# Squares summed on VectorE at the end of layer 0, their statistics between two projections, three banks for the values, other load and block orders

## The chip, the cores and the metric

One core of one Trainium2 chip. The metric is the device time of one launch in microseconds, as the median of several runs.

## What is computed

A transformer of two layers on 512 image tokens and 256 context tokens of 1024 features, all in float32. Each layer normalises, projects to queries, keys, values and a Fourier input, runs three mixers (global attention, a Fourier mix, attention in a window), projects back, and then runs a gated FFN of width 2816. The context is carried along in layer 0 only; in layer 1 it serves keys and values.

```python
def swiglu(h, w_gate, w_up, w_down):
    return (jax.nn.silu(h @ w_gate) * (h @ w_up)) @ w_down

def reference(x, c, ctx, c_ctx, w_ada, ..., g_final):
    rope = axial_rope_tables(x.shape[1])
    for l in range(DEPTH):                                  # DEPTH = 2
        update_ctx = l < DEPTH - 1
        sh1, sc1, gt1, sh2, sc2, gt2 = ...adaln(c, w_ada[l], b_ada[l])
        h = rms_norm(x, g_mix[l]) * (1 + sc1) + sh1
        hc = rms_norm(ctx, g_mix[l]) * (1 + csc1) + csh1
        qa, ka, va, fb, qc, kc, vc = mixer_inputs(h, w_in[l], q_norm[l], k_norm[l], rope)
        qac, kac, vac, fbc, qcc, kcc, vcc = mixer_inputs(hc, w_in[l], q_norm[l], k_norm[l], None)
        o = concatenate([global_attention(qa, ka, va, kac, vac), fourier_mix(fb),
                         window_attention(qc, kc, vc, kcc, vcc, sink[l])])
        x = x + gt1 * (o @ w_out[l])
        x = x + gt2 * swiglu(rms_norm(x, g_ffn[l]) * (1 + sc2) + sh2, w_gate[l], w_up[l], w_down[l])
        if update_ctx:
            ...                                             # the same for ctx
    return rms_norm(x, g_final)
```

## The kernel before

**Arithmetic.** Every float32 product is three passes of a reduced format: each operand is split into a high part and a remainder, and high times high, high times low and low times high are summed in PSUM. `split` (L95) makes the high part with a cast on ScalarE and the low part with a subtraction on VectorE; `mm3` (L89) issues the three matmuls for each pair of operands. Because both are helpers, most rows of the profile carry L89 or L95, and the names of the tiles tell the steps apart: `w` split weights, `raw` weights as loaded, `u` the product of gate and up (and other temporary tiles), `ahi`/`alo` the normalised activations, `th`/`tl` sums of them.

**Large products by seven.** The output projection and the FFN multiply 2 by 2 blocks with seven products in place of eight. The operands' sums are made on GpSimd and VectorE (`seven`, L1269 to L1313). In layer 0 the FFN keeps `u`: parts of it are written to DRAM as `uh` and `uf` and read back, and the seven products with `w_down` come at the end in the order 1, 6, 2, 7, 5, 4, 3, each over eleven panels `k` (`product`, L1453; matmuls L1462). Product 1 needs the blocks of `w_down` in `a11`; `a21` and `a22` are loaded meanwhile, and `sums_of` turns the three into the operands of later products on VectorE.

**PSUM.** There are eight banks in three pools: `lg` two tiles of two banks, `mm` three banks, `fl` one bank. A matmul that starts a new tile waits until the last reader of the tile before in that bank is done.

**The end of layer 0.** `add` (L1471) puts a finished output block into the residual `xt`, and `stat_add` squares it on ScalarE into one of two buffers `sq` and adds the square to `acc`. `stat` (L399, L400) then sums over the features with one-column matmuls, `bc` takes the reciprocal root (GpSimd, L314) and spreads it by a matmul with the identity (L413); `norm_h` makes the normalised `u` on VectorE (L430), `ahi` on ScalarE (L433) and `alo` on VectorE (L434). The tokens come in two halves of 384: the half with block 3 and the context's blocks 4 and 5 (a block is 128 tokens) is finished and normalised during product 3, the half with blocks 0 to 2 after it. The next layer's first projection of block 3 (`qkv_first`, L487 to L489) is computed in between, and the context's blocks 4 and 5 (`qkv_ctx`) after the statistics.

**Layer 1's start.** `qkv_rest` computes `va` (the values of the global attention) in three products, each in a bank handed over as an argument, then the other columns, of which `kc` also uses `fl`. Keys are rotated (L667 to L669), transposed (L589) and cast to `K1a`; queries are transposed (L750); L792 and L800 are the logits.

**Layer 1's FFN.** Eleven panels of 256 columns. Each panel runs `seven` for the gate and for up, multiplies (L1623) and splits the result `u`, in two halves `j`, and one panel later `down` multiplies it by `w_down` into `mm`, eight output blocks of six matmuls (two `j` by three).

**What sets the order.** A scheduler orders the instructions of each engine ahead of time from the order of the code and modelled times; each engine then works through its list strictly in order. `issue_after` pins what is written under it behind a named instruction. SyncE's queue issues nearly all the loads.

Of the kernel before, what the change touches and what calls it, by code (L numbers as in the profile page):

```python
# [17 lines left out]
P = 128  # L18
D = 1024
KB = D // P  # L20
# [26 lines left out]
class Builder:  # L47
# [30 lines left out]
    def mm(self):  # L78
        return self.mmp.tile([P, 512], F32, name=self.nm("mm"), tag="mm")
# [5 lines left out]
    def mm3(self, out, pairs, more=False):  # L85

        n = len(pairs)
        for i, (lh, ll, rh, rl) in enumerate(pairs):
            mm = lambda a, b, **k: self.nc.tensor.matmul(out, a, b, skip_group_check=more, **k)  # L89
            mm(lh, rh, start=(i == 0 and not more), stop=False)  # L90
            mm(lh, rl, start=False, stop=False)
            mm(ll, rh, start=False, stop=(i == n - 1))

    def split(self, hi, lo, src):
        return self.nc.scalar.copy(hi, src).ins, self.nc.vector.tensor_sub(lo, src, hi).ins  # L95
# [295 lines left out]
    def stat(self, acc, rng, ps=None):  # L391

        nc = self.nc
        r0, r1 = rng
        n = (r1 - r0) // P
        ps = self.mm() if ps is None else ps
        for t in range(n):
            o = ps[:, t : t + 1]
            nc.tensor.matmul(o, acc[:, r0 + t * P : r0 + (t + 1) * P], self.ones, start=True, stop=False)  # L399
            nc.tensor.matmul(o, self.lastsq[:, t * P : (t + 1) * P], self.ones, start=False, stop=True)  # L400
        return ps[:, 0:n]

    def stat_bc(self, acc, rng, bank=None, ps=None):
# [108 lines left out]
    def qkv_ctx(self, hi, lo, ws, h0):  # L512

        cs = slice(h0 * HD, 512)
        outs = []
        for tb in range(TBX, TB):
            ts = slice(tb * P, (tb + 1) * P)
            ps = self.mm()
            self.mm3(
                ps[:, cs], [(hi[k][:, ts], lo[k][:, ts], ws[k][0][:, cs], ws[k][1][:, cs]) for k in range(KB)]  # L520
            )
            outs.append(ps)
        return outs

    def qkv_a(self, l, hi, lo, ws, outs):

# [488 lines left out]
    def mix(self, l, hi, lo, ws, outs):  # L1015
        nc = self.nc
        full = l < DEPTH - 1
        self.qkv_tiles(full)
        krs, rms, turn = self.qkv_a(l, hi, lo, ws, outs)
        va = self.qkv_rest(l, hi, lo, "va", self.fl, self.mm, self.fl)  # L1020
        va.pop(0)()

        if full:
# [352 lines left out]
    def ffn_full(self, l, xt, hs):  # L1376
        nc = self.nc
        wg, wu = (self.a[k][l] for k in ("w_gate", "w_up"))
        wd = self.a["w_down"][l].rearrange("(p i q) c -> q p i c", i=2, q=P)
        npc = FB // 2  # L1380
# [37 lines left out]
        half = (slice(0, 512), slice(512, 1024))  # L1418
        a11 = [r[k // 4][:, k % 4] for k in range(8)] + t2[0:3]
        a22 = t2[3 : 3 + npc]  # L1420
        a21 = [act(i) for i in range(npc)]
        for k in range(0, 8, 2):
            nc.sync.dma_start(r[k // 4][:, k % 4 : k % 4 + 2], wd[:, k : k + 2, 0, half[0]])
        turn = [0]
# [46 lines left out]
        def add(v, d, r0, last=False):  # L1471

            for x0, x1, s in ((r0, min(SX, r0 + n), 0), (max(SX, r0), r0 + n, 1)):
                if x0 < x1:
                    nc.vector.scalar_tensor_tensor(
                        xt[d][:, x0:x1], v[:, x0 - r0 : x1 - r0], self.gt(l, 1, d, s), xt[d][:, x0:x1], op0=ALU.mult, op1=ALU.add
                    )
            if last:
                h = r0 // n
                self.stat_add(acc, xt[d], (r0, r0 + n), seen[h], nc.gpsimd)  # L1480
                seen[h] += 1

        def sums_of(k):

            nc.sync.dma_start(a21[k], wd[:, k, 0, half[1]])
            nc.sync.dma_start(a22[k], wd[:, k, 1, half[1]])
            nc.vector.tensor_sub(a11[k], a11[k], a21[k])
            nc.vector.tensor_add(a21[k], a21[k], a22[k])
            nc.vector.tensor_sub(a22[k], a22[k], a11[k])
# [4 lines left out]
        def behind(k):  # L1494

            if k + 4 in range(8, npc):
                nc.sync.dma_start(a11[k + 4], wd[:, k + 4, 0, half[0]])
            if k >= 4:
                sums_of(k - 4)

        half4 = range(4)
        A = [(self.mm() if i else self.fl())[:, 0:n] for i in half4]
        product(1, A, then=behind)
        for k in range(npc - 4, npc):
            sums_of(k)
        s1 = [t[:, i * n : (i + 1) * n] for t in [self.utile(F32) for _ in range(2)] for i in range(2)]
        for i in half4:
            nc.scalar.copy(s1[i], A[i])
# [45 lines left out]
        self.qkv_first(hi, lo, ws, outs, (3,))  # L1554
        for i in half4:
            add(A[i], i, n2, True)
        bc = self.stat_bc(acc, (0, n), self.fl(), self.mm())
        outs += self.qkv_ctx(hi, lo, ws, KB - 2)
        for d in (4, 5, 6, 7, 0, 1, 2, 3):
            nc.sync.dma_start(self.xsc[:, d, 0:SX], xt[d][:, 0:SX])  # L1560
        self.norm_h(hi, lo, xt, bc, (0, n), l + 1, 0, 0, room)
# [3 lines left out]
    def ffn(self, l, xt, hs):  # L1565
# [12 lines left out]
        def down(p, us, rng, s, wd2, ds=range(KB)):  # L1578
            r0, r1 = rng
            last = p == npc - 1  # L1580
            for d in ds:
                ps = self.mm()[:, 0 : r1 - r0]
                c = slice(d * P, (d + 1) * P)
                self.mm3(
                    ps,
                    [
                        (wd2[j][0][:, c], wd2[j][1][:, c], us[j][0][:, r0:r1], us[j][1][:, r0:r1])
                        for j in (1, 0)
                    ],
                )  # L1590
# [15 lines left out]
        for p in range(1, npc):  # L1606
            g = [self.utile(F32) for _ in range(2)]
            self.seven(wg[:, cols(p)], toks, n, *g, lambda o, ps: nc.scalar.activation(o, ps, AF.Silu))
            for t in (g[0][:, n : 2 * n], both(g[1])):
                nc.scalar.activation(t, t, AF.Silu)  # L1610
            wd2 = load_down(p - 1)
            down(p - 1, us, XR, 0, wd2)
            if full:
                down(p - 1, us, CR, 1, wd2)
            m = [self.utile(F32) for _ in range(2)]
            self.seven(
                wu[:, cols(p)], toks, n, *m, lambda o, ps: nc.vector.tensor_tensor(o, ps, g[0][:, 0:n], op=ALU.mult)
            )
            us = utiles()
            if p < npc - 1:  # L1620
                for j in (1, 0):
                    e = slice(0 if j else n, 2 * n)
                    nc.vector.tensor_tensor(m[j][:, e], m[j][:, e], g[j][:, e], op=ALU.mult)  # L1623
                    v = (lambda t: both(t).rearrange("p (i n) -> p i n", i=2)) if j else both
                    self.split(v(us[j][0]), v(us[j][1]), swap(m[j]) if j else both(m[j]))
                continue
            for h in range(2):
                for j in range(2):
                    a = slice((h ^ j) * n, ((h ^ j) + 1) * n)
                    o = slice(h * n, (h + 1) * n)  # L1630
                    if h or j:
                        nc.vector.tensor_tensor(m[j][:, a], m[j][:, a], g[j][:, a], op=ALU.mult)
                    self.tail = self.split(us[j][0][:, o], us[j][1][:, o], m[j][:, a])
# [179 lines left out]
```

## Time and profile before

| | |
|---|---|
| runs | 1590.9, 1590.29, 1589.07 us; median 1590.29 |
| the profiled execution | 1590.55 us, span 1588.8 us |
| mean granted TensorE clock | 0.976 |
| busy: TensorE, VectorE, ScalarE, GpSimd | 95%, 71%, 48%, 37% |
| context blocks, statistics and block 3 at layer 0's end | about 904 to 935 us |
| start of layer 1 up to its first logits | about 935 to 978 us |
| layer 1's FFN | about 1190 to 1566 us |
| product 1 of layer 0's `w_down` | about 735 to 755 us |

PE is TensorE, PEld its weight loads, DVE VectorE, ACT ScalarE, POOL GpSimd, SP SyncE. A timeline row has start, duration (of the whole row, where several instructions are gathered, "x6"), engine, line, operation, output and inputs, and in brackets the idle time before it and what ended it. A row of a group has its total and the mean of one in ns. The clock column is the share of the full TensorE clock that was granted.

### The profile page before, as it was taken

The page shows a single profiled execution, that of the slowest core. Times are in us where ns is not written, and L with a number is a line of the kernel's source. Part 1 is how long each engine was busy: PE and PEld are TensorE (multiplying, and loading weights), DVE is VectorE, ACT ScalarE, POOL GpSimd, SP SyncE. Part 2 cuts the span into 40 slices and gives each one's busy share as a digit, 9 for nine tenths or more (in the row PEclk, how much of TensorE's full clock was granted, in tenths as well). Part 3 has the DMA queues.
Part 4 walks back from the last instruction along what each step waited for, and adds up shares of the span by engine and source line. Part 5 has one row for each costly group of instructions (what it writes and reads, how often), then busy time and mean ns, then how long its engine had stood idle before and what let it go on. Part 6 is the DMA issues. An engine that isn't in the chain of part 4 may idle for free. (4 is left out here: it accounts for less than half of the span.)

```text
span 1588.8 us, 25749 instructions
## 1 busy us (share of the span) xinstructions
PE 1513.1 (95%) x9817; PEld 1383.3 (87%) x9817; DVE 1133.9 (71%) x1891; ACT 765.6 (48%) x1540; POOL 583.5 (37%) x475
## 2 busy tenths in 40 slices
PE   6989999999999999998999898999899999999997
PEld 3689977688999999998999888987799898988987
DVE  4566577753987788887587645667749777787775
ACT  4356566641744344442355424666627343443434
POOL 2163355410265655551021205453401443344432
PEclk9999999999999999999999979999999999999998
DMA  9420075851044345449973610055441423223221
GB/s 339 151 80 28 1 241 174 290 178 54 27 144 163 127 144 179 138 139 393 310 252 105 186 53 27 28 165 200 150 133 54 133 80 106 81 84 129 80 80 53
DMA packets 124842, 217.75 MB, mean 137 GB/s; under 512 B 6616, under 2 KB 83440, under 8 KB 119600
## 3 DMA queue, kind: packets, MB, share of 16 engines
q1 hardware_dynamic: 116864, 210.08, 38.5%
q0 software_dynamic: 7856, 6.04, 1.9%
q8 instruction: 77, 1.26, 0.3%
q14 instruction: 45, 0.37, 0.1%
HBM read 184.96 MB, written 31.13 MB: 136 GB/s over the span
## 5 line engine op out<-in xcount | busy, mean ns | idle before, releaser
L95 DVE TENSOR_TENSOR w<-raw,w 128x512 fp32r<-128x512 f32 (+1 forms) x334 | 316.5, 960 | 111.8 <-ACT w L95 107.1
L95 ACT CAST w<-raw 128x512 fp32r<-128x512 f32 (+1 forms) x334 | 226.5, 699 | 326.3 <-POOL raw L1277 94.4
L89 PE MATMUL mm<-u,w 128*128 128x512 f32 (+1 forms) x576 | 141.6, 387 | 15.2 <-ACT u L95 11.9
L89 PE MATMUL fl<-ahi,w 128*128 128x384 f32 (+1 forms) x640 | 154.4, 309 | 1.0 <-ACT acc L1338 0.9
L811 POOL TENSOR_TENSOR p<-p,rc 128x768 f32<-128x768 f32 (+2 forms) x84 | 112.2, 1354 | 117.0 <-DVE rc L809 108.4
L89 PE MATMUL lg<-ahi,w 128*128 128x384 f32 (+1 forms) x640 | 151.3, 312 | 1.0 <-DVE u L1300 0.9
L89 PE MATMUL lg<-th,w 128*128 128x384 f32 (+1 forms) x640 | 149.9, 309 | 1.1 <-DVE u L1401 0.7
L89 PE MATMUL fl<-w,ahi 128*128 128x256 f32 (+1 forms) x640 | 125.7, 292 | 5.9 <-DVE t L669 3.1
L89 PEld LDWEIGHTS mm<-u,w 128*128 128x128 f32 x576 | 100.3, 196 | 33.4 <-ACT u L95 13.1
L89 PEld LDWEIGHTS lg<-ahi,w 128*128 128x128 f32 x640 | 112.6, 193 | 5.0 <-ACT w L95 1.7
L89 PEld LDWEIGHTS fl<-ahi,w 128*128 128x128 f32 x640 | 112.1, 189 | 2.8 <-ACT acc L1338 1.1
L89 PEld LDWEIGHTS lg<-th,w 128*128 128x128 f32 x640 | 110.9, 189 | 2.8 <-DVE u L1401 1.1
L89 PEld LDWEIGHTS fl<-w,ahi 128*128 128x128 f32 x640 | 103.8, 197 | 7.7 <-issue 2.7
L89 PE MATMUL mm<-ahi,w 128*128 128x256 f32 (+1 forms) x448 | 107.1, 330 | 0.0
L1277 POOL TENSOR_TENSOR raw<-raw 128x512 f32<-128x512 f32 x40 | 62.2, 1556 | 103.5 <-DVE w L95 103.5
L89 PE MATMUL lg<-alo,w 128*128 128x384 f32 (+1 forms) x320 | 99.2, 311 | 0.0
L89 PE MATMUL fl<-alo,w 128*128 128x384 f32 (+1 forms) x320 | 98.7, 308 | 0.0
L89 PE MATMUL lg<-tl,w 128*128 128x384 f32 (+1 forms) x320 | 98.7, 308 | 0.0
L95 DVE TENSOR_TENSOR t<-mm,t 128x512 fp32r<-128x512 f32 x108 | 74.0, 687 | 33.1 <-ACT t L95 32.2
L1269 POOL TENSOR_TENSOR s<-raw 128x512 f32<-128x512 f32 x40 | 53.0, 1326 | 114.8 <-DMA raw<-in_w_up_dram 71.0
L89 PE MATMUL fl<-w,alo 128*128 128x256 f32 (+1 forms) x320 | 92.8, 290 | 0.0
L803 DVE TENSOR_REDUCE neg<-lg 128x1 f32<-128x768 f32 (+2 forms) x96 | 81.0, 852 | 14.6 <-PE lg L800 13.4
(352 smaller groups left out, 3957.8 us busy)
## 6 DMA issues: line engine op xcount, KB each, us to landing
raw<-in_w_ada_dram SPq DMA_DIRECT2D x40, 1024.0 KB, 4.9
raw<-in_w_gate_dram SPq DMA_DIRECT2D x22, 1024.0 KB, 5.2
raw<-in_w_up_dram SPq DMA_DIRECT2D x22, 1024.0 KB, 5.2
uh<-uh SPq DMA_DIRECT2D x44, 384.0 KB, 5.3
w<-uh SPq DMA_DIRECT2D x44, 384.0 KB, 4.6
wd<-in_w_down_dram SPq DMA_DIRECT2D x58, 256.0 KB, 5.4
raw<-in_w_down_dram SPq DMA_DIRECT2D x11, 1024.0 KB, 4.8
raw<-in_w_in_dram SPq DMA_DIRECT2D x10, 1024.0 KB, 6.2
```

The lines of the kernel that those rows point to most:

```text
L89: mm = lambda a, b, **k: self.nc.tensor.matmul(out, a, b, skip_group_check=more, **k)
L95: return self.nc.scalar.copy(hi, src).ins, self.nc.vector.tensor_sub(lo, src, hi).ins
L803: nc.vector.tensor_reduce(ng, lv, axis=AX.X, op=ALU.max, negate=True)
L811: nc.gpsimd.tensor_tensor(pt, pt, rc[:, i : i + 1].to_broadcast(list(pt.shape)), op=ALU.mult)
L1269: nc.gpsimd.tensor_add(s1, a21, a22)
L1277: nc.gpsimd.tensor_sub(a12, a12, a11)
```

## The change

1. **Adds of squares.** At the end of layer 0 the twelve adds of squares into `acc` (three after each of products 2, 5, 4 and 3) run on VectorE, not on GpSimd.
2. **Statistics between the context's blocks.** `qkv_ctx` hands over one block at a time. Block 4 comes first, then `stat`, pinned behind its last matmul, then block 5, pinned behind `stat`, then `bc`.
3. **Banks for the values in layer 1.** The three products of `va` go to `mm`, `lg` and `fl` instead of `fl`, `mm` and `fl`.
4. **Loads of w_down in layer 0.** `a21` is loaded four panels behind product 1 as before, but `a22` and the sums come six behind; and the tiles behind `a21` are taken in another order.
5. **Order of the halves.** In layer 1's FFN half `j` = 0 comes before half 1, both in the multiply and split of `u` and in the six matmuls of each `down` block.

```diff
-            mm(ll, rh, start=False, stop=(i == n - 1))
+            self.last = mm(ll, rh, start=False, stop=(i == n - 1)).ins
...
     def qkv_ctx(self, hi, lo, ws, h0):
...
-            outs.append(ps)
-        return outs
+            yield ps
...
-        va = self.qkv_rest(l, hi, lo, "va", self.fl, self.mm, self.fl)
+        va = self.qkv_rest(l, hi, lo, "va", *((self.fl, self.mm, self.fl) if full else (self.mm, self.lg1, self.fl)))
...
-        a21 = [act(i) for i in range(npc)]
+        a21 = [act(i) for i in (0, 1, 2, 3, 8, 9, 10, 4, 5, 6, 7)]
...
-                self.stat_add(acc, xt[d], (r0, r0 + n), seen[h], nc.gpsimd)
+                self.stat_add(acc, xt[d], (r0, r0 + n), seen[h])
...
         def sums_of(k):
 
-            nc.sync.dma_start(a21[k], wd[:, k, 0, half[1]])
             nc.sync.dma_start(a22[k], wd[:, k, 1, half[1]])
...
-            if k >= 4:
-                sums_of(k - 4)
+            if 4 <= k < npc + 4:
+                nc.sync.dma_start(a21[k - 4], wd[:, k - 4, 0, half[1]])
+            if k >= 6:
+                sums_of(k - 6)
...
-        for k in range(npc - 4, npc):
-            sums_of(k)
+        for k in range(npc, npc + 6):
+            behind(k)
...
-        bc = self.stat_bc(acc, (0, n), self.fl(), self.mm())
-        outs += self.qkv_ctx(hi, lo, ws, KB - 2)
+        ctx = self.qkv_ctx(hi, lo, ws, KB - 2)
+        outs.append(next(ctx))
+        with self.tc.issue_after(self.last):
+            ss = self.stat(acc, (0, n), self.mm())
+        with self.tc.issue_after(self.last):
+            outs.append(next(ctx))
+        bc = self.bc(ss, n // P, self.fl())
...
-                        for j in (1, 0)
+                        for j in range(2)
...
-                for j in (1, 0):
+                for j in range(2):
                     e = slice(0 if j else n, 2 * n)
                     nc.vector.tensor_tensor(m[j][:, e], m[j][:, e], g[j][:, e], op=ALU.mult)
```

How the instructions move. TensorE's list has the same number of matmuls in both kernels. At the end of layer 0 (`lg_9330` is the projection of block 3, of which only the last panel and a half is left; `mm_9371` before and `mm_9395` after hold the statistics; `mm_9370` is context block 4 after, `mm_9385` before) it reads before:

```order
L489 MATMUL lg_9330<-w_9323,alo_9034 128x512 [waits DVE_49]
L487 MATMUL lg_9330<-w_9323,ahi_9027 128x512 [waits Activation_49]
L488 MATMUL lg_9330<-w_9324,ahi_9027 128x512
L489 MATMUL lg_9330<-w_9323,alo_9035 128x512 [waits DVE_49]
L399 MATMUL mm_9371<-ones,acc_7581 128x1 [waits Pool_49]
L400 MATMUL mm_9371<-ones,sq_9368 128x1 [waits Activation_49]
```

And after, where nineteen more rows of `mm_9370` stand ahead of the first row shown:

```order
L89 MATMUL mm_9370<-w_9324,ahi_9026 128x128
L491 MATMUL lg_9330<-w_9323,alo_9034 128x512 [waits DVE_49]
L489 MATMUL lg_9330<-w_9323,ahi_9027 128x512 [waits Activation_49]
L490 MATMUL lg_9330<-w_9324,ahi_9027 128x512
L89 MATMUL mm_9370<-w_9323,alo_9034 128x128 [waits DVE_49]
L89 MATMUL mm_9370<-w_9323,ahi_9027 128x128 [waits Activation_49]
L89 MATMUL mm_9370<-w_9324,ahi_9027 128x128
L491 MATMUL lg_9330<-w_9323,alo_9035 128x512 [waits DVE_49]
L89 MATMUL mm_9370<-w_9323,alo_9035 128x128 [waits DVE_49]
L399 MATMUL mm_9395<-ones,acc_7581 128x1 [waits DVE_49]
L400 MATMUL mm_9395<-ones,sq_9368 128x1 [waits Activation_49]
```

All of block 4 now stands between the projection of block 3 and the statistics, which wait for VectorE in place of GpSimd. (Lines after are two higher here: L489 to L491 for L487 to L489.)

At layer 1's start on TensorE before (`fl_9757` is the third product of `va`, `fl_10072` the first of `kc`, both in the one `fl` bank):

```order
L89 MATMUL fl_9757<-w_9576,ahi_9027 128x256
L89 MATMUL fl_9757<-w_9577,ahi_9027 128x256
L89 MATMUL fl_9757<-w_9576,alo_9035 128x256
L89 MATMUL fl_10072<-w_10001,ahi_9020 128x256 [waits DVE_49,PE_49,Activation_49]
L89 MATMUL fl_10072<-w_10002,ahi_9020 128x256
```

And after, where `lg_9814` is a product of `va`:

```order
L89 MATMUL fl_10072<-w_10005,ahi_9027 128x256
L89 MATMUL fl_10072<-w_10006,ahi_9027 128x256
L89 MATMUL fl_10072<-w_10005,alo_9035 128x256
L89 MATMUL lg_9814<-w_9572,ahi_9020 128x256 [waits DVE_49,Activation_49]
L89 MATMUL lg_9814<-w_9573,ahi_9020 128x256
```

The products of `kc` have moved ahead of two of `va`, which now start in another bank.

In layer 1's FFN, at the first `down` block after a panel's product 4 of the gate, on TensorE (`u_13218` and `u_13219` are the high and low part of half 0, `u_13220` and `u_13221` of half 1; `mm_13365` and `mm_13373` the first two output blocks; `lg_13440` the next panel's first product, `w_13434` its weights) before:

```order
L89 MATMUL mm_13365<-u_13220,w_13361 128x512 [waits Activation_49]
L89 MATMUL mm_13373<-u_13220,w_13361 128x512 [waits DVE_49]
L89 MATMUL lg_13440<-ahi_9020,w_13434 128x256 [waits Activation_49]
L89 MATMUL lg_13440<-alo_9028,w_13434 128x256
L89 MATMUL mm_13365<-u_13221,w_13361 128x512 [waits DVE_49]
L89 MATMUL mm_13365<-u_13220,w_13362 128x512
```

And after:

```order
L89 MATMUL mm_13365<-u_13218,w_13357 128x512 [waits Activation_49]
L89 MATMUL mm_13365<-u_13219,w_13357 128x512 [waits DVE_49]
L89 MATMUL mm_13365<-u_13218,w_13358 128x512 [waits DVE_49]
L89 MATMUL mm_13373<-u_13218,w_13357 128x512 [waits DVE_49]
L89 MATMUL mm_13373<-u_13219,w_13357 128x512
L89 MATMUL mm_13373<-u_13218,w_13358 128x512
L89 MATMUL lg_13440<-ahi_9020,w_13434 128x256 [waits Activation_49]
L89 MATMUL lg_13440<-alo_9028,w_13434 128x256
L89 MATMUL mm_13365<-u_13220,w_13361 128x512 [waits Activation_49]
```

Six matmuls of half 0 stand ahead of the next panel's first product where two of half 1 stood. On ScalarE the cast of half 0 now comes before the two casts of `w_down`, and that of half 1 behind the cast of the next panel's weights `w_13434`, which waits for their load. Before, that cast stood behind half 1's:

```order
L95 CAST w_13337<-raw_13230 128x512 [waits DVE_49,PE_49]
L95 CAST w_13357<-raw_13355 128x1024 [waits DMAHW5_49,PE_49]
L95 CAST w_13361<-raw_13355 128x1024 [waits DVE_49,PE_49]
L95 CAST u_13220<-u_13094 128x512 [waits DVE_49,Pool_49]
L95 CAST w_13434<-raw_13431 128x512 [waits DMAHW6_49,PE_49,Activation_49]
L95 CAST u_13218<-u_13093 128x512
```

And after:

```order
L95 CAST w_13337<-raw_13230 128x512 [waits DVE_49,PE_49]
L95 CAST u_13218<-u_13093 128x512 [waits DVE_49]
L95 CAST w_13357<-raw_13355 128x1024 [waits DMAHW5_49,PE_49]
L95 CAST w_13361<-raw_13355 128x1024 [waits PE_49,Activation_49]
L95 CAST w_13434<-raw_13431 128x512 [waits DMAHW6_49,PE_49,Activation_49]
L95 CAST u_13220<-u_13094 128x512 [waits DVE_49,Pool_49]
```

Half 0's cast moves from last to second.

More of the change, by code (lines that the diff above doesn't have):

```diff
@@ L399, in stat @@
             nc.tensor.matmul(o, acc[:, r0 + t * P : r0 + (t + 1) * P], self.ones, start=True, stop=False)
-            nc.tensor.matmul(o, self.lastsq[:, t * P : (t + 1) * P], self.ones, start=False, stop=True)
+            self.last = nc.tensor.matmul(
+                o, self.lastsq[:, t * P : (t + 1) * P], self.ones, start=False, stop=True
+            ).ins
         return ps[:, 0:n]
@@ L514, in qkv_ctx @@
         cs = slice(h0 * HD, 512)
-        outs = []
         for tb in range(TBX, TB):
```

## The prediction

> **What bounds the kernel now.** I read the page first, then the waits of TensorE, then single stretches as windows and timelines.
>
> ```profile
> PE 1513.1 (95%) x9817; PEld 1383.3 (87%) x9817; DVE 1133.9 (71%) x1891; ACT 765.6 (48%) x1540; POOL 583.5 (37%) x475
> ...
> PE mm L89 <- ACT u L95: 11.9, 6, 3.5
> PE fl L1462 <- DMA w<-uh: 6.3, 1, 6.3
> ...
> PE mm L89 <- DVE u L95: 3.2, 7, 0.7
> PE fl L89 <- DVE t L669: 3.1, 3, 2.5
> ```
>
> TensorE is busy 95% of the span and runs almost the same matmuls after the edit, so only its idle time and the time at a lower clock can be won. The waits (total us, times, longest) name three groups near the edited code: the halves of `u` in layer 1's FFN (11.9 + 3.2 us), the spilled `uh` load in product 1 (6.3) and the `fl` bank at layer 1's start (3.1). A fourth, the sum of squares at layer 0's end, is in the timeline below. The windows add the clock (columns: stretch, its length, busy time of PE, PEld, DVE, ACT, POOL, clock, DMA share, GB/s).
>
> ```profile
> 740.00:746.40 6.40, 0.08 (x2) 0.03 (x1) 6.40 (x11) 0.62 (x1) 0.39 (x1) 0.78 1.05 393
> 746.40:750.40 4.00, 4.00 (x13) 4.00 (x14) 4.00 (x8) 0.00 (x0) 0.00 (x0) 0.50 1.04 414
> 800.00:830.00 30.00, 30.00 (x175) 30.00 (x174) 26.27 (x49) 16.43 (x33) 11.10 (x3) 1.00 0.80 269
> 912.20:934.70 22.50, 22.50 (x92) 21.24 (x93) 9.28 (x21) 4.73 (x10) 2.22 (x3) 0.50 0.01 3
> 960.00:966.00 6.00, 4.06 (x21) 4.09 (x22) 1.80 (x9) 0.00 (x0) 6.00 (x6) 0.72 0.01 3
> 1364.00:1368.00 4.00, 3.82 (x24) 3.12 (x24) 2.86 (x4) 2.30 (x5) 0.65 (x1) 1.00 0.94 305
> ```
>
> After a gap of some us the clock is 0.50 for a few us (746.4 to 750.4), and once, from 912.2 to 934.7, for 22.5 us although PE was busy in all of them. A full cold spell of 3.4 us (the length I read off the short ones) costs 1.7 us. The gap length that triggers one lies, by the stretches here, somewhere near 2 us.
>
> **The end of layer 0.**
>
> ```profile
> 906.95 0.50 PE L489 MATMUL lg<-w,alo 128*128 128x512 f32 x1 [2.09 <-DVE alo L434]
> 912.14 0.59 PE L399 MATMUL mm<-ones,acc 128*128 128x1 f32 x2 [3.49 <-POOL acc L389]
> 914.72 0.67 PE L89 MATMUL mm<-w,ahi 128*128 128x128 f32 x2
> 919.66 1.59 PE L413 MATMUL fl<-ident,rs 128*128 128x128 f32 x6
> 926.28 0.73 PE L487 MATMUL lg<-w,ahi 128*128 128x512 f32 x1
> 928.09 0.52 PE L89 MATMUL fl<-w,ahi 128*128 128x128 f32 x2
> 930.54 0.73 PE L489 MATMUL lg<-w,alo 128*128 128x512 f32 x1
> 906.67 5.41 POOL L389 TENSOR_TENSOR acc<-acc,sq 128x384 f32<-128x384 f32 x3 [20.58 <-ACT sq L385]
> 907.87 1.22 DVE L95 TENSOR_TENSOR w<-raw,w 128x1024 fp32r<-128x1024 f32 x1
> 921.29 4.29 DVE L430 SCALAR_TENSOR_TENSOR u<-xt,smod,fl 128x384 f32<-128x384 f32 x8 [6.24 <-PE fl L413]
> 921.94 4.29 ACT L433 ACTIVATE ahi<-u,ada 128x384 fp32r<-128x384 f32 x8 [10.37 <-DVE u L430]
> L389 POOL TENSOR_TENSOR acc<-acc,sq 128x384 f32<-128x384 f32 x12 | 25.0, 2082 | 140.8 <-ACT sq L385 140.2
> L1307 DVE TENSOR_TENSOR u<-u,lg 128x384 f32<-128x384 f32 x20 | 11.0, 550 | 10.1 <-PE lg L89 10.0
> L385 ACT ACTIVATE sq<-xt 128x384 f32<-128x384 f32 x14 | 7.1, 521 | 7.1 <-POOL acc L389 4.9 <-DVE xt L1475 2.1
> ```
>
> The chain to `stat` is square, add, square, add. On GpSimd the three last adds end at 906.67 + 5.41 = 912.08 and `stat` starts at 912.14. The new adds have no row; the nearest is VectorE's add of the same shape, L1307 at 0.55 us. They stand in VectorE's order behind the split of `w` that ends at 907.87 + 1.22 = 909.09. The third add needs a square (0.52) made in the buffer that the first frees: 909.09 + 0.55 + 0.52 + 0.55 is about 910.75, and `stat` starts near 910.85, 1.3 us earlier. Meanwhile TensorE runs twenty matmuls of context block 4 where it idled 2.09 us (its bank comes free with the first of the L1475 adds), then the rest of block 3, and is done near 908.1: the gap before `stat` falls from 3.49 to some 2.7 us. I take it that this still drops the clock, since six one-column matmuls and narrow ones follow.
>
> From there, all at half speed: `stat` takes 2.58 (912.14 to 914.72) and ends at 913.4. Block 5's 24 matmuls at 0.213 us (23 in 919.66 - 914.72 = 4.94, with a little slack) end at 918.5, and `bc`'s six at 1.24 end near 919.8; GpSimd's reciprocal root is ready long before. Here the cover runs out. VectorE must now make the first `u` and ScalarE its `ahi`: in the rows `bc` ends near 920.9, the first `ahi` near 922.5, and the eighth `u`, which frees `fl`, at 921.29 + 4.29 = 925.58. With the same lags the wide L489 matmuls start at 921.4, four of them end near 923.2, and the twelve narrow `fl` matmuls (928.09 to 930.54, 2.45 us) start when `fl` is freed at 919.8 + 4.7 = 924.5, ending at 926.95 against 930.54. **Gain 3.6 us**; two new idle stretches (1.6 and 1.3 us) are in it. Bounds: 1.3 us, the shift of `stat` alone, and about 9 if the clock stays up: `stat` and block 5 then end at 914.7, `bc` at 915.3, `fl` is freed at 920.0, and the twelve end at 921.3.
>
> The nine other adds of squares fall in products 7, 5 and 4. There VectorE is busy 26.27 of 30 us (800 to 830), PE 30 of 30. Three adds are 1.65 us a product. The splits run up to five steps ahead of TensorE (ten `w`/`u` slots, two a step), which are five times twelve matmuls of 30.00/175 = 0.17 us, some 10 us: cost 0. Without that lead each three would cost 1.65, in all 5 us.
>
> **Layer 1's start.**
>
> ```profile
> 961.94 0.67 PE L89 MATMUL fl<-w,ahi 128*128 128x256 f32 x2 [2.54 <-DVE t L669]
> 977.01 0.63 PE L750 MATMUL mm<-ident,qax 128*128 128x128 f32 x4 [0.96 <-DVE t L669]
> 977.64 0.50 PE L792 MATMUL lg<-K1a,qt 128*128 128x512 f32 x1
> 969.17 0.41 POOL L583 TENSOR_TENSOR kr<-y,rs 128x128 f32<-128x128 f32 x1
> 975.97 1.17 ACT L596 CAST K1a<-mm 64x512 fp32r<-64x512 f32 x2
> ```
>
> With `va` in `mm`, `lg` and `fl`, the third product of `va` no longer sits in the only `fl` bank ahead of the next one. The 2.54 us before 961.94 go, as the new order puts 48 matmuls into `lg` there, whose bank the rotary sums of the projection free at about that time. The cold spell after it (0.72 in the 960 to 966 row; 1.7 us) goes too. TensorE alone would reach the logits at 977.64 - 2.54 - 1.7 - 0.96 = 972.4. But they need the last `kr` (969.58), its transposes and casts of `K1a` (1.17), queued on ScalarE among casts of `w`. I estimate 975: **gain 2.5 us**, between 5.2 (no such limit) and -1 (a new gap there with a cold spell of its own, and `lg` freed late).
>
> **Order of the halves in layer 1's FFN.**
>
> ```profile
> 1329.76 0.42 DVE L1313 TENSOR_TENSOR u<-u,mm 128x256 f32<-128x256 f32 x1 [0.63 <-POOL u L1308]
> 1331.51 1.29 POOL L1269 TENSOR_TENSOR s<-raw 128x512 f32<-128x512 f32 x1 [1.79 <-DMA raw<-in_w_up_dram]
> 1331.66 0.73 PE L89 MATMUL mm<-u,w 128*128 128x512 f32 x2 [1.67 <-ACT u L95]
> 1333.41 2.36 PE L89 MATMUL mm<-u,w 128*128 128x512 f32 x6 [0.69 <-DVE u L95]
> 1400.60 1.65 PE L89 MATMUL mm<-u,w 128*128 128x512 f32 x6 [0.63 <-DVE u L95]
> 1257.61 1.07 DVE L1623 TENSOR_TENSOR u<-u,u 128x256 f32<-128x256 f32 x1
> 1265.38 0.85 PE L89 MATMUL mm<-u,w 128*128 128x512 f32 x2 [3.48 <-ACT u L95]
> 1265.55 1.64 POOL L1269 TENSOR_TENSOR s<-raw 128x512 f32<-128x512 f32 x1 [3.13 <-DMA raw<-in_w_up_dram]
> 1266.85 2.65 PE L89 MATMUL mm<-u,w 128*128 128x512 f32 x6
> 1562.59 5.34 PE L89 MATMUL mm<-u,w 128*128 128x256 f32 x30 [1.77 <-ACT u L95]
> ```
>
> At every second panel TensorE runs dry before the first `mm<-u`. Half 1 of `u` ends a long chain (product 7, L1307, GpSimd's L1308, L1313, L1623); half 0 had its product at 1257.61, but its cast stood last. Now half 0 goes first: six matmuls at 0.23 us (the warm six of 1400.60 take about 1.4; two banks, of which the second waits for L1313, done at 1330.18) fill 1330.0 to 1331.4. The next weights land at 1331.5 in either case; their cast (0.62) lets two `lg` through to 1332.5, and half 1's cast, now behind it, two `mm` to 1333.2. The same ten matmuls ended at about 1335.5 before (1333.41 plus six): 2.3 us, or 1.6 at the two like 1400.60, where the six ran warm. At 1265 the load lands late, at 1265.5: the six run to 1263.6 and the rest ends at 1267.7 instead of 1269.5, 1.8 us. Two of 2.3, two of 1.6 and 1.8 are 9.6. I take **9 us**, since the second bank may come later; bounds 4.6 (only the four extra matmuls of 0.23 us fill each of five gaps) and 12 (two cold spells that outlast the six matmuls end as well). The boundaries between these idle little (3.82 of 4.00 us busy at 1364 to 1368): 0. In the last panel six `mm<-u` of 5.34/30 = 0.18 us move ahead into the 1.77 us before 1562.59: between 0 and 1.1, I take 0.5.
>
> **Loads of w_down.** The order shows the same transfers in the same places on SP's queue; only which `k` a tile holds changes, and the VectorE sums come two steps later. The 6.4 us at 740 belong to a saturated DMA (1.05) and stay. Cost 0, bounds -2 and +2 (half of the cold spell that follows it).
>
> **Sum.** 3.6 + 2.5 + 9 + 0.5 = 15.6. The profiled execution took 1590.55 us (span 1588.8), 0.26 above the median of the runs shown, so 1575.
>
> A rule against the trace: the Trainium skill, page "TensorE: Matmul & The Clock Gate", Part 1, says that the full clock comes back after one busy window of about 3.4 us. The row 912.20:934.70, 22.50 us busy and still at 0.50, disagrees, so the sum keeps the long cold stretch.
>
> **Rivals.**
> 1. The clock returns inside the narrow matmuls, once TensorE has been busy for 3.4 us. Then block 5 ends near 917.8, `bc` at 918.5, the twelve at 924.5, and the 4.2 us of cold work after 930.54 go (2.1): layer 0's end gives 8, in all 1570.5. Against it: the 22.5 us row. Chance 0.04. (By that rule of the skill's page this would be the forecast; the trace does not bear it out.)
> 2. The clock never drops before `stat`, since block 4 fills most of the gap. 9 instead of 3.6 there, 1569.5. For it: the gap is 2.7 us instead of 5.6 in two pieces; against: one of 2.54 us sufficed at 959. Chance 0.10.
> 3. Other releasers take over: `stat` gives only 1.3, the logits wait until 977.6, and in the FFN the second bank or the weight load holds all but the four matmuls. 1590.55 - 1.3 - 4.6 = 1584.6, and 1588 where these too are halved. For it: the weight load lands within 0.2 us of the old cast. Chance 0.17, of which 0.07 lies within 0.2% of before, about what a measurement tells from no change (3.2 us).
> 4. Slower: the adds on VectorE tie ScalarE to VectorE. A square waits for its buffer, that for an add behind splits, those for casts queued behind the square. If this circle eats the 10 us lead in products 7, 5 and 4 and then holds TensorE, it decides from 5.2 us a product (15.6 in three); at 6.3 us each the time is 1590.55 - 15.6 + 19 = 1594. For it: VectorE's 26.27 of 30. Against: GpSimd's adds, at 2.08 us, made the same waits without a PE gap. Chance 0.07.
>
> The forecast itself: 0.62, its own range 1569 to 1581. Faster 0.62 + 0.10 + 0.04 + 0.10 = 0.86, same 0.07, slower 0.07. The range 1566 to 1586 leaves out rival 4, the upper half of rival 3 and some 0.04 below: 0.19.
>
> **What would show it.** After: POOL L389 gone from layer 0; `stat` 1 to 1.5 us earlier relative to the end of product 3, still at 0.50; no `fl<-w,ahi` wait of 2.5 us on L669; the waits for ACT `u` and DVE `u` at the five boundaries down from 15 to under 6 us, with fewer cold spells; the 6.3 us wait on `uh` unchanged. It is wrong if a gap of over 2 us stands before layer 1's logits, if `mm<-u` still waits 1.7 us on ACT, or if products 7, 5 or 4 show idle time.

## The result and the profile after

The changed kernel takes 1575.24 us in the median of four runs (1574.51 to 1576.13) against 1589.68 for the kernel before (four runs, 1587.55 to 1590.9). The ratio is 0.9911, 95% interval 0.9894 to 0.9928: 14.2 us faster, 11.4 to 16.9. The forecast was 1575, 1566 to 1586. The profiled execution has a span of 1574.4 us. Two executions further down, one of 5115.9 us (the profiled one of e1_halves) and one of 2088.91 us (e4_loads), took far longer than all others and stand in none of the ratios and tables.

The line of engines of the kernel after, and some of its waits of TensorE (total us, times, longest):

```profile
PE 1504.6 (96%) x9817; PEld 1376.2 (87%) x9817; DVE 1128.7 (72%) x1903; ACT 763.8 (49%) x1540; POOL 557.4 (35%) x463
...
PE fl L1462 <- DMA w<-uh: 6.2, 1, 6.2
...
PE lg L89 <- ACT w L95: 3.3, 5, 2.2
...
PE mm L750 <- DVE t L669: 2.8, 1, 2.8
...
PE lg L89 <- DVE w L95: 2.7, 4, 0.7
...
PE mm L89 <- DVE u L95: 2.5, 3, 0.8
...
PE mm L399 <- DVE acc L389: 1.9, 1, 1.9
```

The wait for `uh` is where it was. The long waits of `mm<-u` for ScalarE, 11.9 us in all before, are gone from the head of the list. Their wait for VectorE's part of `u` went from 3.2 to 2.5 us, and two that were not in the list before stand beside it (`lg` for `w`, 3.3 us on ScalarE and 2.7 on VectorE). The wait of 2.54 us at the `fl` bank is gone, and one of 2.77 us at L750 is new.

The end of layer 0, timeline of TensorE after (lines are two higher than before):

```profile
912.36 0.38 PE L399 MATMUL mm<-ones,acc 128*128 128x1 f32 x2 [1.88 <-DVE acc L389]
917.46 1.59 PE L415 MATMUL fl<-ident,rs 128*128 128x128 f32 x6
920.40 0.79 PE L489 MATMUL lg<-w,ahi 128*128 128x512 f32 x1 [1.35 <-ACT ahi L435]
923.52 0.66 PE L89 MATMUL fl<-w,ahi 128*128 128x128 f32 x2 [1.05 <-DVE u L432]
926.11 0.73 PE L491 MATMUL lg<-w,alo 128*128 128x512 f32 x1
```

And two windows of it (stretch, length, busy time of PE, PEld, DVE, ACT and POOL, clock, DMA share, GB/s):

```profile
912.40:915.20 2.80, 2.80 (x25) 2.80 (x26) 0.16 (x1) 0.00 (x0) 0.85 (x1) 1.00 0.48 180
915.40:928.80 13.40, 11.00 (x40) 9.24 (x40) 9.12 (x20) 4.62 (x10) 0.65 (x1) 0.50 0.00 0
```

Sequence and gaps in the timeline are those that the prediction worked out: one gap ahead of the statistics, one behind `bc` (1.35 us, waiting for the first `ahi`) and one until the eighth `u` frees `fl` (1.05). The windows say that the statistics and the first part of block 5 still run at the full clock (1.00); then it is 0.50 for 13.4 us, where it was 0.50 for 22.5 before.

To compare kernels by stretches I use three marks that all of them have: the first matmul of product 1 that waited for `uh`, the one that waited for the first `Va`, and the FFN's first wait, for `acc`. Before these rows are:

```profile
746.40 1.30 PE L1462 MATMUL fl<-w,w 128*128 128x384 f32 x3 [6.32 <-DMA w<-uh]
...
953.39 0.50 PE L89 MATMUL fl<-w,ahi 128*128 128x256 f32 x2 [1.07 <-DVE Va L95]
...
1225.95 0.39 PE L89 MATMUL fl<-ahi,w 128*128 128x256 f32 x1 [0.94 <-ACT acc L1338]
```

And after:

```profile
748.13 1.30 PE L1462 MATMUL fl<-w,w 128*128 128x384 f32 x3 [6.20 <-DMA w<-uh]
...
948.32 0.51 PE L89 MATMUL fl<-w,ahi 128*128 128x256 f32 x2 [1.07 <-DVE Va L95]
...
1221.71 0.39 PE L89 MATMUL fl<-ahi,w 128*128 128x256 f32 x1 [0.94 <-ACT acc L1338]
```

The first stretch (products of `w_down`, the end of layer 0) fell from 206.99 to 200.19 us, the second (layer 1's mixers) rose from 272.56 to 273.39, the third (from there to the span's end) fell from 362.85 to 352.69. The first mark itself lies behind work that no part touches, and yet between 746.40 and 751.76 us in the thirteen profiled executions that the table at the end of the experiments lists: single executions differ by that much before the edited code begins.

### The profile page after: what moved, and what is told of

It is laid out like the page before. It is cut to its first block, busy times and chain, and to the rows that moved or that the text cites. A ratio compares the mean times of both kernels' runs of the same rounds, so it can differ in the third digit from the quotient of the medians.

```text
span 1574.4 us, 25728 instructions
## 1 busy us (share of the span) xinstructions
PE 1504.6 (96%) x9817; PEld 1376.2 (87%) x9817; DVE 1128.7 (72%) x1903; ACT 763.8 (49%) x1540; POOL 557.4 (35%) x463
## 4 chain that ended last, share of the span: by engine, by line
PE 68%; DVE 11%; DMA 8%; POOL 5%; issue 4%; ACT 4%; SPq 0%; POOLq 0%; DVEq 0%; ACTq 0%
PE mm L89 15%; PE fl L89 12%; PE lg L89 11%; DVE w L95 5%; PE lg L1462 4%; PE mm L904 4%; PE mm L1462 3%; PE fl L254 3%; DMA raw<-in_w_up_dram 2%; PE mm L896 2%; ACT w L95 2%; PE lg L792 2%; PE lg L800 2%; POOL raw L1277 1%; PE fl L1462 1%
## 5 line engine op out<-in xcount | busy, mean ns | idle before, releaser
L95 DVE TENSOR_TENSOR w<-raw,w 128x512 fp32r<-128x512 f32 (+1 forms) x334 | 307.0, 931 | 119.2 <-ACT w L95 114.3
L89 PE MATMUL mm<-u,w 128*128 128x512 f32 (+1 forms) x576 | 137.4, 377 | 3.8 <-DVE u L95 2.5
L314 POOL TENSOR_TENSOR rs<-ms,mhalf 128x8 f32<-128x8 f32 (+3 forms) x22 | 27.6, 1260 | 319.0 <-DVE ms L312 319.0
L89 PE MATMUL fl<-w,ahi 128*128 128x256 f32 (+1 forms) x608 | 119.9, 292 | 4.1 <-DVE w L95 1.5
L89 PEld LDWEIGHTS fl<-w,ahi 128*128 128x128 f32 x608 | 98.6, 197 | 5.9 <-DVE w L95 1.8
```

## The experiments

Each kernel was timed in rounds beside the kernel before; the ratio's interval is 95%. Three theories stand behind them: the parts add up as the marks of one pair of profiles show them; the prediction's own sizes hold; or it decides where the spells of low clock fall. Lines that are left out of a diff are marked with three dots.

**e1_halves: part 5 alone.**

```diff
-                        for j in (1, 0)
+                        for j in range(2)
...
-                for j in (1, 0):
+                for j in range(2):
```

> Before with part 5 alone (order of the halves). Theory 1, the parts add up: between the first matmuls of layer 1's FFN and the end the changed kernel won 10.2 us against before (4.24 us ahead at its first waits, 14.4 at the end), so 10 us here, 1579.5, with the waits of mm<-u for ACT and DVE down from 15 to about 4 us. Theory 2, the prediction's bound: only the four moved matmuls of each boundary count, 4.6 us, 1585.

Measured: 0.9958 (0.9943 to 0.9974), 6.7 us faster (4.1 to 9.1). The first theory's 10 us are excluded: the marks of one pair of profiles had overstated the part. The second's 4.6 us lie inside the interval.

**e2_stat: parts 1 and 2 alone.**

```diff
...
-                self.stat_add(acc, xt[d], (r0, r0 + n), seen[h], nc.gpsimd)
+                self.stat_add(acc, xt[d], (r0, r0 + n), seen[h])
...
-        bc = self.stat_bc(acc, (0, n), self.fl(), self.mm())
-        outs += self.qkv_ctx(hi, lo, ws, KB - 2)
+        ctx = self.qkv_ctx(hi, lo, ws, KB - 2)
+        outs.append(next(ctx))
+        with self.tc.issue_after(self.last):
+            ss = self.stat(acc, (0, n), self.mm())
+        with self.tc.issue_after(self.last):
+            outs.append(next(ctx))
+        bc = self.bc(ss, n // P, self.fl())
```

> Before with parts 1 and 2 alone (adds on VectorE, statistics between the context's blocks). Theory 1: the marks of the changed kernel stood 5.9 us earlier at the wide matmuls behind the narrow ones, against its own lead ahead of product 1; all of it comes here, 5 to 6 us, 1584. Theory 2: the 2.3 us above the predicted 3.6 came from where the clock's windows happened to fall (in the changed kernel the clock was still full through the statistics), and this kernel gives 3.6 or less, 1586.

Measured: 0.9958 (0.9944 to 0.9973), 6.7 us faster (4.3 to 8.9), which excludes the second theory's 3.6. Its profiled execution alone would have spoken for that theory: it took 204.23 us in the first stretch, 2.8 less than before and 4.0 more than the changed kernel, with the same code at layer 0's end. The windows show why:

```profile
914.00:933.80 19.80, 17.40 (x65) 15.16 (x65) 9.28 (x21) 4.62 (x10) 2.21 (x3) 0.50 0.02 7
```

Here the clock is down for 19.8 us, from the middle of the statistics (which start at 913.03), against 13.4 us after. Where the spell starts within the statistics differs between executions of one sequence.

**e3_banks: part 3 alone.**

```diff
-        va = self.qkv_rest(l, hi, lo, "va", self.fl, self.mm, self.fl)
+        va = self.qkv_rest(l, hi, lo, "va", *((self.fl, self.mm, self.fl) if full else (self.mm, self.lg1, self.fl)))
```

> Before with part 3 alone (banks for the values). Theory 1: the 2.5 us gap at the fl bank is gone, and a new one of some 2.8 us at the transposes of the queries takes its place, as in the changed kernel: 0 to +1 us, 1590. Theory 2, the prediction: 2.5 us faster, 1587.

Measured: 1.0005 (0.9994 to 1.0016), no change that can be told; the 2.5 us are excluded. Its timeline shows the new waits:

```profile
976.49 1.09 PE L750 MATMUL mm<-ident,qax 128*128 128x128 f32 x4 [4.06 <-DVE t L669]
...
981.85 0.51 PE L89 MATMUL fl<-w,ahi 128*128 128x256 f32 x2 [1.78 <-DVE t L669]
```

**e4_loads: part 4 alone.**

```diff
-        a21 = [act(i) for i in range(npc)]
+        a21 = [act(i) for i in (0, 1, 2, 3, 8, 9, 10, 4, 5, 6, 7)]
...
-            nc.sync.dma_start(a21[k], wd[:, k, 0, half[1]])
             nc.sync.dma_start(a22[k], wd[:, k, 1, half[1]])
...
-            if k >= 4:
-                sums_of(k - 4)
+            if 4 <= k < npc + 4:
+                nc.sync.dma_start(a21[k - 4], wd[:, k - 4, 0, half[1]])
+            if k >= 6:
+                sums_of(k - 6)
...
```

> Before with part 4 alone (loads of w_down). Theory 1: the 6.2 us wait for uh stays and nothing else moves, within 0.5 us of before. Theory 2: the sums come out of the way of the splits in product 1 and 1 to 2 us are won in products 1 and 6, 1588.

Measured: 1.0002 (0.9988 to 1.0015): no change that can be told, as forecast; the second theory's 1 to 2 us are not seen, though 1.9 is the interval's edge. The parts alone give 6.7 + 6.7 - 0.8 - 0.3 = 12.3 us, the whole 14.2 (11.4 to 16.9): within what the intervals allow, they add up.

**e5_adds: part 1 alone.**

```diff
-                self.stat_add(acc, xt[d], (r0, r0 + n), seen[h], nc.gpsimd)
+                self.stat_add(acc, xt[d], (r0, r0 + n), seen[h])
```

> Before with part 1 alone (the twelve adds of squares on VectorE, statistics in their old place). Theory 1, by the prediction's rows: stat starts 1.3 us earlier and everything behind it follows at half clock, 1.3 us faster, 1588. Theory 2: both parts are needed for any of the 6.7 us of e2, since only block 4 in front of the statistics keeps the clock up; 0. Theory 3: VectorE's adds delay the splits in products 7, 5 and 4: slower by 2 us or more.

Measured: 0.9988 (0.9976 to 1.0), 1.9 us faster (0 to 3.8). That fits the first theory and excludes the third; the second's 0 is the edge of the interval. In its trace, too, no wait of TensorE stands between 755 and 905 us, so the adds on VectorE do not hold it up in the products.

**e6_order: part 2 alone.**

```diff
...
-        bc = self.stat_bc(acc, (0, n), self.fl(), self.mm())
-        outs += self.qkv_ctx(hi, lo, ws, KB - 2)
+        ctx = self.qkv_ctx(hi, lo, ws, KB - 2)
+        outs.append(next(ctx))
+        with self.tc.issue_after(self.last):
+            ss = self.stat(acc, (0, n), self.mm())
+        with self.tc.issue_after(self.last):
+            outs.append(next(ctx))
+        bc = self.bc(ss, n // P, self.fl())
```

> Before with part 2 alone (statistics between the context's blocks, adds still on GpSimd). Theory 1: stat stays at its old time (912.1), held by GpSimd, but block 4 stands in the gap ahead of it and no longer in the cold stretch; block 5, bc, the eight u and the twelve narrow matmuls then end 2.3 us earlier, and with some full clock through the statistics 4: 1586 to 1587. Theory 2: the order is everything, 6 us, 1583.

Measured: 0.9984 (0.9968 to 0.9999), 2.5 us faster (0.2 to 5.1), with a wait of 3.08 us for GpSimd ahead of the statistics. The first theory fits, the second's 6 us are excluded. Each half of the pair is worth about 2 us; the intervals leave open whether the two together (6.7) give more than their sum (4.4).

**e7_fill: unread matmuls in the gap before the statistics of the changed kernel.** Their results are used nowhere, so the kernel does ten matmuls more.

```diff
+        sb = self.mm()
+
+        def idle(m):
+            for _ in range(m):
+                with self.tc.issue_after(self.last):
+                    self.last = nc.tensor.matmul(
+                        sb[:, P:512], hi[0][:, SX - P : SX], ws[0][0][:, 0:384], start=True, stop=True
+                    ).ins
+
+        idle(10)
         with self.tc.issue_after(self.last):
-            ss = self.stat(acc, (0, n), self.mm())
+            ss = self.stat(acc, (0, n), sb)
```

> The changed kernel with ten matmuls of 128x384 more, whose results are read by nobody, in the gap between context block 4 and stat (1.7 us at full clock in a gap of 1.9). If the gap lets the clock drop: the clock stays full through stat, block 5 and bc, which end 1.8 us earlier than in the changed kernel, and with them all behind: 1573 against 1575.2. If the clock goes down for another reason (one-column or narrow matmuls): 1575 to 1576 and the same stretch at 0.50.

Measured: 0.9938 (0.9922 to 0.9954), 1577.94 us where before took 1587.08 beside it, 9.8 us faster (7.3 to 12.4): no more than the changed kernel gains over its own before (r9_again below, 0.9932), so the first theory's 1573 is not reached. The windows answer the question on the clock:

```profile
913.50:916.80 3.30, 3.21 (x23) 2.86 (x21) 2.34 (x4) 1.05 (x2) 0.00 (x0) 1.00 0.91 296
916.80:920.10 3.30, 3.30 (x32) 3.30 (x31) 0.16 (x1) 0.00 (x0) 0.85 (x1) 1.00 0.20 76
920.30:933.60 13.30, 10.90 (x35) 8.66 (x34) 9.12 (x20) 4.62 (x10) 1.36 (x2) 0.50 0.00 0
```

The gap is filled, TensorE is busy for 6.5 us of 6.6, block 5 runs at full clock, and at about 920.2 the clock drops all the same. So the statistics and block 5 do run faster (`bc` 4.1 us behind the statistics' start, 5.1 in the changed kernel's profile), but no gap is needed for the clock to fall: it falls behind a stretch of one-column and 128-column matmuls without any.

**e8_fill2: fourteen more behind bc.**

```diff
-            nc.tensor.matmul(
+            self.lastbc = nc.tensor.matmul(
...
         bc = self.bc(ss, n // P, self.fl())
+        self.last = self.lastbc
+        idle(14)
```

> As e7_fill, with fourteen more such matmuls between bc and the next wide matmuls (2.4 us at full clock where the changed kernel idles 1.35 and 1.05 us). If gaps set the clock: no cold stretch at layer 0's end at all, the wide matmuls behind run at full speed, 4.5 us faster than the changed kernel, 1571. If the narrow ones set it: 1576 to 1578, since the extra matmuls run at half speed.

Measured: 0.9937 (0.9922 to 0.9952), 1577.37 us, 10.0 us faster than before (7.6 to 12.4), so the first theory's 1571 is not reached either. In the windows the clock drops as in e7, but is back after 3.4 us:

```profile
916.40:919.60 3.20, 3.20 (x30) 3.20 (x30) 0.16 (x1) 0.00 (x0) 0.85 (x1) 1.00 0.15 54
919.80:923.00 3.20, 3.20 (x13) 3.20 (x14) 1.79 (x4) 1.14 (x3) 0.00 (x0) 0.50 0.00 0
923.20:936.00 12.80, 12.59 (x64) 10.53 (x63) 8.92 (x19) 5.40 (x10) 1.36 (x2) 1.00 0.19 63
```

The first stretch takes 197.63 us, 2.6 less than in the changed kernel's profile. In the total this does not appear; with intervals of 2 to 3 us it is left open whether it is lost later or only not seen.

**r9_again: the changed kernel beside the next three.** No edit.

> The changed kernel once more, beside the next three. 14 us faster than before, 0.991. Where its FFN runs are like e7 and e8, the stretch from the FFN's first wait for the sum acc to the end is 353 to 357 us against 358.6 to 362.9 in the five kernels with the old order of halves.

Measured: 0.9932 (0.9912 to 0.9952), 1575.47 us where before took 1587.19. That is 10.8 us faster (7.6 to 14.0), less than the 14.2 (11.4 to 16.9) of the first comparison; the 12.3 of the parts lie between the two. The third stretch took 352.85 us.

**r10_oldbanks: the changed kernel without part 3.**

```diff
-        va = self.qkv_rest(l, hi, lo, "va", *((self.fl, self.mm, self.fl) if full else (self.mm, self.lg1, self.fl)))
+        va = self.qkv_rest(l, hi, lo, "va", self.fl, self.mm, self.fl)
```

> The changed kernel without part 3 (values in fl, mm, fl as before). Theory 1: the banks are worth nothing or cost a little (the gap moves from the fl bank to the queries' transposes): the same as the changed kernel or up to 1.5 us faster, since the stretch from the first product of va to the FFN took 273.4 us in the mean of the kernels with the new banks and 271.9 with the old ones. Theory 2, the prediction: 2.5 us slower than the changed kernel.

Measured: 0.9906 (0.9891 to 0.9922), 1572.70 us, its five runs (1571.59 to 1573.52) all below the six of r9_again (1574.23 to 1583.32): 2.8 us by the medians, so the second theory is out. The waits at the start of layer 1 are:

```profile
955.67 0.47 PE L89 MATMUL fl<-w,ahi 128*128 128x256 f32 x2 [1.74 <-DVE ms L312]
...
970.08 0.63 PE L750 MATMUL mm<-ident,qax 128*128 128x128 f32 x4 [1.80 <-DVE t L669]
```

The two add up to 3.54 us, as much as with the same banks before (2.54 + 0.96), so the old banks wait no less than they did. What differs from the changed kernel is the clock behind them (columns as above). In the changed kernel's profile:

```profile
972.28:975.69 3.41, 3.41 (x14) 3.17 (x14) 3.32 (x7) 2.35 (x4) 0.76 (x2) 0.50 0.00 0
```

It falls in that of r9_again too, from about 977.4. In that of r10_oldbanks it does not:

```profile
972.28:975.69 3.41, 3.07 (x26) 3.02 (x26) 3.28 (x6) 2.53 (x4) 0.73 (x1) 1.00 0.00 0
```

Why the clock falls behind one wait of 2.77 us and not behind two of under 2, no run here shows. In the table below the second stretch takes 271.7 us in the mean of the seven executions with the old banks and 273.5 in the five with `mm`, `lg` and `fl`. This version is the fastest that was measured.

**r11_lglg: the values in lg, lg and fl.**

```diff
-        va = self.qkv_rest(l, hi, lo, "va", *((self.fl, self.mm, self.fl) if full else (self.mm, self.lg1, self.fl)))
+        va = self.qkv_rest(l, hi, lo, "va", *((self.fl, self.mm, self.fl) if full else (self.lg1, self.lg1, self.fl)))
```

> The changed kernel with the three products of va in lg, lg and fl. The four transposes that waited 2.77 us for the rotary sums of the product in mm now find a free bank. If that bank was the cause, the wait at L750 goes, and the logits start 1 to 2 us earlier, 1 us faster than the changed kernel. If the chain on ScalarE and VectorE (two casts and two subtractions of w ahead of the sums) is, the same wait appears at the logits, whose lg banks the same sums free, and the time stays.

Measured: 0.9931 (0.9912 to 0.9949), 1576.83 us, as r9_again. The eight transposes run without a wait, and the wait stands at the logits:

```profile
965.49 1.04 PE L750 MATMUL mm<-ident,qax 128*128 128x128 f32 x8
970.13 1.19 PE L792 MATMUL lg<-K1a,qt 128*128 128x512 f32 x2 [3.38 <-DVE qt L761]
```

Between these two layouts, then, the bank is only the place where the wait shows. What ends it is VectorE, and the changed kernel's rows say what it does meanwhile:

```profile
964.44 1.05 ACT L95 CAST w<-raw 128x1024 fp32r<-128x1024 f32 x1 [3.93 <-PE mm L89]
965.98 1.05 ACT L95 CAST w<-raw 128x1024 fp32r<-128x1024 f32 x1 [0.49 <-PE mm L89]
...
967.06 1.23 DVE L95 TENSOR_TENSOR w<-raw,w 128x1024 fp32r<-128x1024 f32 x1 [0.32 <-ACT w L95]
968.20 0.42 DVE L95 TENSOR_TENSOR Va<-mm,Va 128x256 fp32r<-128x256 f32 x1
968.53 0.41 DVE L667 TENSOR_TENSOR t<-mm,cst 128x256 f32<-128x256 f32 x1
...
969.49 0.70 PE L750 MATMUL mm<-ident,qax 128*128 128x128 f32 x4 [2.77 <-DVE t L669]
```

The rotary sums (L667 to L669) stand in VectorE's order behind the split of the next weights, which needs ScalarE's casts, and the first of these casts had itself waited 3.93 us for TensorE. In r11_lglg `qt` stands behind the same split. This is read from the traces; no run moves the split.

**r12_fill_oldbanks: e8_fill2 without part 3.** The edit of e8_fill2 and that of r10_oldbanks together.

> e8_fill2 (unread matmuls in both gaps at layer 0's end) without part 3. If the clock's cold stretch is worth the 3.6 us that e8's marks show from product 3 to the first product of va, and the old banks cost nothing, 3 to 5 us faster than the changed kernel in this call. If the phase of the clock's windows eats it later, the same as the changed kernel.

Measured: 0.9915 (0.9898 to 0.9931), 1574.94 us: not faster than r10_oldbanks, and not the first theory's 3 to 5 us faster than r9_again, though its first stretch was 197.83 us against 200.24. Its third was 357.00 against 352.54, with one more cold spell in the FFN in that execution. The unread matmuls are not shown to be worth anything.

The stretches of the profiled executions, all but that of e1_halves, worked out from the marks as above (us):

| | product 1 to first Va | first Va to FFN | FFN to end |
|---|---|---|---|
| before | 206.99 | 272.56 | 362.85 |
| e4_loads | 206.18 | 273.09 | 361.12 |
| e3_banks | 206.53 | 274.61 | 360.66 |
| e5_adds | 204.30 | 271.37 | 358.57 |
| e6_order | 202.98 | 270.89 | 359.97 |
| e2_stat | 204.23 | 271.41 | 360.28 |
| after | 200.19 | 273.39 | 352.69 |
| r9_again | 204.35 | 274.02 | 352.85 |
| r10_oldbanks | 200.24 | 271.24 | 352.54 |
| r11_lglg | 200.31 | 271.92 | 353.99 |
| e7_fill | 201.17 | 271.50 | 356.99 |
| e8_fill2 | 197.63 | 273.98 | 354.03 |
| r12_fill_oldbanks | 197.83 | 271.60 | 357.00 |

## Why the prediction was right, and where its terms were not

The time fell on the forecast because errors of the terms cancelled, which is luck. The sum was 15.6 us; 14.2 (11.4 to 16.9) were measured, and 10.8 (7.6 to 14.0) in r9_again. By kernels with one part each, and parts 1 and 2 together:

| term | forecast | measured |
|---|---|---|
| end of layer 0 (parts 1, 2) | 3.6 (1.3 to 9) | 6.7 (4.3 to 8.9) |
| layer 1's start (part 3) | 2.5 (-1 to 5.2) | -0.8 (-2.5 to 1.0); 2.8 us faster without it in the changed kernel |
| order of the halves and last panel (part 5) | 9 + 0.5 (4.6 to 12) | 6.7 (4.1 to 9.1) |
| loads of w_down (part 4) | 0 (-2 to 2) | -0.3 (-2.4 to 1.9) |

**End of layer 0.** The order of events was right: the statistics wait for VectorE, block 4 fills most of the gap (1.88 us are left, forecast 2.7), and behind `bc` the chain of `u` and `ahi` takes over with gaps of 1.35 and 1.05 us (forecast 1.6 and 1.3). The step that failed is "this still drops the clock", which I let happen before the statistics. It happens 0.5 to 3 us after their start, by execution. Nor do the runs show a gap length that sets it, for which the working had "somewhere near 2 us": behind gaps of 1.86 and 1.88 us the clock held for another 0.5 us (e2_stat) or 3 us (after), and in e7_fill it fell without a gap. In five executions of the same sequence the first stretch took 204.23 and 204.35 us with 19.5 us or more at 0.50, and 200.19, 200.24 and 200.31 with some 13.5. The row of the second of them, r9_again:

```profile
916.00:935.50 19.50, 17.10 (x65) 15.06 (x65) 9.28 (x21) 4.62 (x10) 2.21 (x3) 0.50 0.04 15
```

Against the mean of before, e3_banks and e4_loads (206.6) that is 2.3 or 6.3 us: the 3.6 lies between two values that occur. Most of the gain is clock: from before to after, TensorE's idle time in the first stretch fell by 0.9 us (6.65 to 5.74), its time at 0.50 from about 31 to 17 (in windows of 1 us).

**Layer 1's start.** The failed step is "they need the last `kr`, its transposes and casts of `K1a`" as the only limit behind the `fl` bank, and with it the 2.5 us. I had the casts of `w` on ScalarE in the count for `K1a`, but not the rotary sums of the product in `mm`, which wait behind them and VectorE's subtractions and hold four transposes for 2.77 us. The sign by which I would know it ("a gap of over 2 us") came out; a cold spell followed (0.50 in the row 972.28:975.69 above). That is the lower end of the term's bounds, not its middle.

**Order of the halves.** Right in mechanism, too large. At the boundaries before I counted 1.67 + 0.69 us of idle time and let most of it go. At the one whose last row the prediction shows (1400.60, idle 0.63 before it) the row ahead is:

```profile
1398.94 0.73 PE L89 MATMUL mm<-u,w 128*128 128x512 f32 x2 [1.67 <-ACT u L95]
```

The rows of the same boundary after:

```profile
1389.27 0.39 PE L89 MATMUL mm<-u,w 128*128 128x512 f32 x1
1390.47 1.43 PE L89 MATMUL mm<-u,w 128*128 128x512 f32 x5 [0.81 <-DVE u L95]
1392.12 0.39 PE L89 MATMUL lg<-ahi,w 128*128 128x256 f32 x1 [0.22 <-ACT w L95]
1393.30 0.51 PE L89 MATMUL lg<-ahi,w 128*128 128x256 f32 x2 [0.68 <-DVE w L95]
```

The six matmuls do run ahead, but the second of them waits 0.81 us for the low part of half 0, which I had taken as ready, and the next product waits 0.22 and 0.68 for the high and the low part of its weights: 1.71 us of idle time for 2.30 (1.67 + 0.63), where my times left some 0.7 ahead of that product (1331.4 to about 1332.1). All in all the third stretch takes 354.3 us in the mean of the seven executions with the new order and 360.6 in the six with the old one, 6.3 us, which agrees with the timed 6.7. Of these, 3.5 us are idle time (21.9 against 18.4 us in the same means). The rest must be clock, as the matmuls are the same: counted in windows of 1 us, it is at 0.50 for about 9 us of the stretch in the mean, where it was for about 17. That the smaller gaps are what spares these spells is likely, but no run holds the gaps and moves the clock.

**Loads, adds in the products.** Both costed at nothing, and neither measured as anything that can be told; no wait of TensorE stands between 755 and 905 us in either profile.

**Rivals.** The first (the clock returns inside the narrow matmuls) did not come: 0.50 from 915.4 to 928.8. The second (the clock stays up before the statistics) came true in its condition, but it was worth 6.7 us and not 9, since the clock falls soon after. Of the third, the weight load does hold part of the FFN's gain: at the boundary above the cast of the next weights, which starts at 1391.45, had waited 2.98 us for their load. The fourth (VectorE's adds stall the splits) fell with e5_adds.

## What to carry to other kernels

A bank that is waited for need not be the cause, as here: follow its last reader's engine back, and see what that engine does ahead of it, before counting the bank's wait as won. A moved wait is worth the difference to the next one, so each operand of the moved instructions (here the low part as well as the high one) needs its own time of readiness. Where the clock falls at another place in each execution, judge terms by several executions: one pair of profiles overstated the FFN's part by half.

## What the runs showed of the hardware

TensorE does not keep its clock here merely by being busy. In e7_fill the row 916.80:920.10 has 3.30 of 3.30 us busy at 1.00 with one-column and 128-column matmuls, and the clock is 0.50 from 920.2. In r12_fill_oldbanks, where the gap is filled as well, it falls at 916.1, inside block 5. In the kernel before, the row 912.20:934.70 stays at 0.50 though busy throughout, all but some 6 us of it with matmuls of at most 128 columns. In e8_fill2 the row 919.80:923.00, likewise 3.20 of 3.20 busy but from 920.83 on with 384-column matmuls, ends with the clock coming back.

The Trainium skill, page "TensorE: Matmul & The Clock Gate", Part 1, puts the low state down to an idle window; the row of e7_fill disagrees, and that of e8_fill2 agrees with its recovery after one busy window. What counts as activity, no run here separates further.
